# A two-layer mixer trunk on one core: the selection's last step moves to ScalarE, the first mean square to VectorE, and every operation gets a new place in the order

## The chip, the cores and the metric

The kernel runs on one core of a Trainium2 chip. The metric is the device time of one execution in microseconds (us), lower is better. The core has five engines with their own instruction queues: TensorE (PE in the profile; its weight loader is shown apart as PEld), VectorE (DVE), ScalarE (ACT), GpSimd (POOL) and SyncE (SP), which in this kernel issues nearly all transfers.

## The reference, cut to what matters

```python
D_MODEL, SEQ, DEPTH = 1024, 512, 2      # batch 1, float32

def rmsnorm(x, g):
    return x * lax.rsqrt(jnp.mean(x * x, axis=-1, keepdims=True) + EPS) * g

def dsa_mixer(q, k, v, qi, ki, wi):                     # group A, per block of 128 queries
    logits = einsum('bqhd,bsd->bqhs', qib, ki) * IDX_DIM ** -0.5
    score = einsum('bqhs,bqh->bqs', relu(logits), wib)  # 8 index heads
    score = where(causal, score, -inf)
    _, idx = lax.top_k(score, 128)                      # min(256, 512 // 4)
    s = einsum('bqhd,bqkd->bhqk', qb, k[idx]) * HEAD_DIM ** -0.5
    return einsum('bhqk,bqkd->bqhd', masked_softmax(s), v[idx])

def hybrid_layer(x, ...):
    p = split_cols(rmsnorm(x, norm_w) @ w_in)
    o_a = dsa_mixer(...)         # group A: indexer, top-k keys, softmax attention
    o_b = nsa_mixer(...)         # group B: compressed, selected and window attention
    o_c = shortconv_mixer(...)   # group C
    o_d = pool_mixer(...)        # group D
    mixed = concatenate([silu(gate) * o for each group])
    return x + mixed @ w_out

def reference(x, ...):
    for l in range(DEPTH):
        x = hybrid_layer(x, ...)
    return rmsnorm(x, final_norm_w)
```

## The kernel before

The 512 tokens are four tiles of 128 (index `i`, 0 to 3), the 1024 channels eight blocks of 128 (`KC`). Products are float32 done in three parts: each operand is split into a high half (ACT copy to the type fp32r) and a low half (DVE or POOL subtraction, the helper `lo` at L585), and TensorE multiplies high by high, high by low and low by high. So a weight block goes through SP (transfer into a staging tile `st`, four buffers), ACT (`wh`), POOL (`wl`; in the first block partly DVE) and then TensorE; `load_w` (L590) does that for `w_in`, `load_half` (L618) for the halves of `w_out`, whose two parts are both called `w`. The activations are `hT` (normed input, transposed, two halves) and `mT` (the mixed outputs, `mT_884` and `mT_885` the halves in layer 2).

A layer normalizes and transposes its input, projects it (`lin_tok`, `lin_ch`: PSUM banks called `mm`, two of them), runs the four groups, and projects the mixed channels with `w_out`, again into banks `mm`. The other PSUM banks are `s` (two: scores), `tr` (three: transposes) and `pv` (one: value products). In the last layer the residual add (`mm<-mm,x`), the scaling (`xn<-mm,g`) and the sum of squares (`junk<-mm`) read a bank `mm` before it is free for the next tile; `mm_1290` and `mm_1287` are the two column halves of one token tile there, `mm_1318` of the next.

The start (L766, `norm_first`): the first norm's two column halves of a token tile come as two loads of `x`. ACT squares and sums the one, DVE the other, POOL adds the two sums (`ss`) and takes the power -1/2 (`ss<-ss,mhalf`); DVE then scales `x` by quarters of 256 columns into `xn`, with the norm weight spread over the partitions by TensorE (`s<-ident,g_col`, L686), and TensorE transposes the quarters. POOL also fills the constants there (memsets and affine selects: `mask`, `cbias`, `cval`, `es`, `rg` and others).

Selection (L871 and L906, `group_idx` and `topk`): for the token tiles 1 to 3 the index score is built up over eight heads in `acc` (256, 384 or 512 wide). Then 16 rounds of DVE's `MAX8` and `MATCH_REPLACE8` mark the 128 largest by a very negative value, and one POOL instruction turns `acc` into 0 for the marked keys and -1e30 (`NEG`) for the others:

```python
            for _ in range(TOPK // 8):
                V.max(m8, a)
                V.match_replace(a, m8, a, MARK)
            G.tensor_scalar(a, a, -2.0e38, NEG, op0=OP.is_gt, op1=OP.mult)
```

`att_a` (L1172) gives it to `probs` (L1070), where one DVE instruction takes -0.125 times score and key bias together with the smallest element of each row (`pb`, `mn`), and ACT takes exp(-(p) + mn) with the row sums. The first token tile has no selection and uses the causal `mask`. Group B's attention uses `probs` and `probs_joint` too; its block selection goes over `e`, `el` (POOL and ACT), TensorE transposes and `es` (ACT).

What sets the order: nothing is issued as the functions run. `Tape.record` notes every operation with what it must follow, and `Tape.play` (L525) issues them in the sequence of a list written out in the code, `ORDER` (L179 to L447), one number for each of the recorded operations. Each engine gets its operations in that sequence, and `Tape.place` gives a tile the buffer of its pool that has been free longest in that sequence. That is why nearly every row of the profile has line L545, and why rows are told apart by their tiles.

Of the kernel before, what the change touches and what calls it, by code (L numbers as in the profile page):

```python
# [17 lines left out]
P = 128  # L18
# [152 lines left out]
class Engine:  # L171
# [378 lines left out]
def trunk(ctx: ExitStack, tc: tile.TileContext, x, norm_w, w_in, w_out, conv_w, pe_cmp, w_cmp_k, w_cmp_v,  # L550
# [31 lines left out]
    def f(ap):  # L582
        return ap.bitcast(F32)

    def lo(eng, dst, src, hi):  # L585

        eng.tensor_sub(dst, src, f(hi))
# [268 lines left out]
    def layer(l, hT, w_first, norm):  # L856
# [6 lines left out]
        def tk(i):  # L863
            return slice(i * P, (i + 1) * P)
# [607 lines left out]
```

## Time and profile before

| | us |
|---|---|
| runs of the kernel before | 528.71, 528.80, 530.26 |
| median | 528.8 |
| the profiled execution's own time | 530.93 |
| its span, first to last instruction | 528.9 |
| mean granted TensorE clock in it | 0.997 of full speed |

| engine | busy us | instructions |
|---|---|---|
| PE | 516.3 | 2887 |
| PEld | 437.9 | 2887 |
| DVE | 370.0 | 1024 |
| ACT | 332.6 | 821 |
| POOL | 330.8 | 596 |

A row of the timeline reads: start in us, length in us, engine, line, operation, output tile `<-` input tiles (without numbers), shapes, `x` count of instructions in a row, and in brackets the idle time before them with what ended it. A row of the groups reads: line, engine, operation, tiles and shape, count, then busy us and mean ns of one, then the idle time before them with what ended most of it. A row of the chain reads: start, length, what. A row of the waits reads: who waited for whom, total us, times, longest us. A matmul's row is longer than the distance to the next matmul's start, since they are pipelined.

### The profile page before, as it was taken

To read this page: it belongs to the slowest core of one execution; us is meant where nothing else is said; L and a number is where in the kernel's file an instruction comes from. 1 tells how busy PE (TensorE), PEld (TensorE's weight loads), DVE (VectorE), ACT (ScalarE), POOL (GpSimd) and SP (SyncE) were. 2 spreads that over 40 slices of the span, in tenths; PEclk is the share of its full clock that TensorE was granted. 3 is DMA by queue.
4 is the path that set the end of the run, shared out by engine and by line. 5 is a ranking of instruction groups with operands and counts; after the bars stand their busy time and mean duration, and the time that the engine had idled before them with its cause. 6 is when DMAs were issued, how large, how long until landed. Compare 5 with 4: busy or idle time off the path is not lost.

```text
span 528.9 us, 9309 instructions
## 1 busy us (share of the span) xinstructions
PE 516.3 (98%) x2887; PEld 437.9 (83%) x2887; DVE 370.0 (70%) x1024; ACT 332.6 (63%) x821; POOL 330.8 (63%) x596
## 2 busy tenths in 40 slices
PE   8999999999999999999999999999999999999995
PEld 8999988778888877788789998778888887878785
DVE  4525899899848575773453369999999856757523
ACT  5669954564466776774365788657475748675612
POOL 6887852776565946739276875457483876592531
PEclk9999999999999999999999999999999999999998
DMA  8943410763322111306543332165303212031304
GB/s 265 293 116 82 94 35 16 175 152 89 71 52 69 40 42 40 96 34 199 175 140 101 104 92 70 40 161 139 80 15 96 67 46 70 10 103 38 111 9 160
DMA packets 72993, 50.09 MB, mean 95 GB/s; under 512 B 24424, under 2 KB 63472, under 8 KB 72944
## 3 DMA queue, kind: packets, MB, share of 16 engines
q1 hardware_dynamic: 72352, 48.45, 33.7%
q10 hardware_dynamic: 592, 1.05, 0.5%
q8 instruction: 23, 0.38, 0.3%
q14 instruction: 26, 0.21, 0.1%
HBM read 45.29 MB, written 4.19 MB: 94 GB/s over the span
## 4 chain that ended last, share of the span: by engine, by line
PE 73%; DVE 9%; ACT 9%; POOL 3%; issue 2%; DMA 2%; SPq 1%; POOLq 0%; ACTq 0%; DVEq 0%
PE mm L545 53%; PE tr L545 9%; PE s L545 6%; PE pv L545 5%; DVE acc L545 2%; ACT qiT L545 2%; DVE m L545 1%; ACT pb L545 1%; ACT wh L545 1%; POOL cd L545 1%; DVE kTB L545 1%; DMA st<-in_w_out_dram 1%; POOL w L545 1%; SPq L545 1%; DMA x<-in_x_dram 1%
## 5 line engine op out<-in xcount | busy, mean ns | idle before, releaser
L545 PE MATMUL mm<-hT,wh 128*128 128x512 f32 x544 | 172.6, 399 | 0.5 <-ACT wh L545 0.5
L545 POOL TENSOR_TENSOR wl<-st,wh 128x384 fp32r<-128x384 f32 (+4 forms) x140 | 127.7, 936 | 32.8 <-ACT wh L545 25.3
L545 PEld LDWEIGHTS mm<-hT,wh 128*128 128x128 f32 x544 | 100.1, 188 | 20.2 <-ACT wh L545 1.0
L545 PE MATMUL mm<-w,mT 128*128 128x512 f32 (+1 forms) x408 | 101.7, 384 | 1.3 <-ACT junk L545 0.6
L545 PE MATMUL mm<-wh,hT 128*128 128x360 f32 (+3 forms) x480 | 100.5, 309 | 0.3 <-DVE vB L545 0.2
L545 PE MATMUL mm<-hT,wl 128*128 128x512 f32 x272 | 97.4, 401 | 0.2
L545 PEld LDWEIGHTS mm<-w,mT 128*128 128x128 f32 x408 | 71.9, 189 | 16.5 <-ACT junk L545 1.3
L545 PEld LDWEIGHTS mm<-wh,hT 128*128 128x128 f32 x480 | 76.5, 189 | 1.4 <-DVE vB L545 0.7
L545 ACT ACTIVATE wh<-st 128x768 fp32r<-128x768 f32 (+4 forms) x72 | 55.5, 780 | 19.4 <-DMA st<-in_w_in_dram 9.7
L545 ACT ACTIVATE pb<-pb,mn 128x128 f32<-128x128 f32 (+3 forms) x96 | 53.3, 557 | 21.3 <-DVE mn L545 20.5
L545 PE MATMUL mm<-wl,hT 128*128 128x360 f32 (+3 forms) x240 | 62.6, 310 | 0.0
L545 PEld LDWEIGHTS mm<-hT,wl 128*128 128x128 f32 x272 | 50.5, 188 | 9.9 <-POOL wl L545 0.5
L545 DVE MAX8 m<-acc 128x8 f32<-128x512 f32 (+2 forms) x96 | 51.7, 551 | 0.7
L545 DVE MATCH_REPLACE8 acc<-m,acc 128x384 f32<-128x384 f32 (+2 forms) x96 | 51.8, 542 | 0.1
L545 DVE TENSOR_TENSOR pl<-tr,ph 128x512 fp32r<-128x512 f32 x60 | 40.4, 684 | 15.7 <-ACT ph L545 9.3
L545 POOL TENSOR_SCALAR pb<-pb,rs,gt 128x512 f32<-128x512 f32 (+3 forms) x64 | 38.3, 615 | 20.6 <-DVE e L545 7.8
L545 POOL TENSOR_TENSOR w<-st,w 128x512 fp32r<-128x512 f32 x32 | 41.0, 1294 | 11.1 <-issue 7.1
L545 PEld LDWEIGHTS mm<-wl,hT 128*128 128x128 f32 x240 | 41.9, 189 | 0.9 <-ACT hT L545 0.3
L545 PE MATMUL tr<-ident,pb 128*128 128x128 f32 x240 | 41.5, 273 | 0.4 <-ACT es L545 0.4
L545 ACT ACTIVATE ph<-tr 128x512 fp32r<-128x512 f32 x60 | 34.3, 592 | 10.7 <-PE tr L545 10.4
L545 DVE CUSTOM_DVE_ANT_0 pb<-s,mask 128x128 f32<-128x128 f32 (+3 forms) x72 | 32.4, 461 | 10.5 <-PE tr L545 5.5
L545 PEld LDWEIGHTS tr<-ident,pb 128*128 128x128 f32 x240 | 30.5, 140 | 8.7 <-ACT es L545 0.6
(167 smaller groups left out, 867.9 us busy)
## 6 DMA issues: line engine op xcount, KB each, us to landing
st<-in_w_in_dram SPq DMA_DIRECT2D x104, 128.0 KB, 2.7
st<-in_w_out_dram SPq DMA_DIRECT2D x32, 256.0 KB, 3.0
st<-in_w_in_dram SPq DMA_DIRECT2D x28, 256.0 KB, 3.1
x<-in_x_dram SPq DMA_DIRECT2D x16, 256.0 KB, 4.8
st<-in_w_in_dram SPq DMA_DIRECT2D x8, 320.0 KB, 4.6
x1d<-x SPq DMA_DIRECT2D x8, 256.0 KB, 2.6
x<-x1d SPq DMA_DIRECT2D x8, 256.0 KB, 3.7
ws<-in_w_in_dram SPq DMA_DIRECT2D x4, 268.0 KB, 4.8
```

What stands on the lines that cost most here:

```text
L545: getattr(self.engines[op.eng].real, op.name)(*[real(a) for a in op.args], **{k: real(v) for k, v in op.kw.items()})
```

## The change

1. The last step of the selection is one ACT instruction, Relu(1e-8 a + 1e30): the marked keys become 0, the others 1e30, with the sign turned round. So group A's keys `kTA` are stored negated, `probs` takes +0.125 for group A, and the first token tile uses a new tile `hide` (0 or 1e30) in the place of a slice of `mask`. `far` is a new column of 1e30.
2. In `norm_first` DVE squares and sums both column halves, the second beginning with the sum of the first. ACT's Square and POOL's add go.
3. All of `ORDER` is new.

```diff
     mask = const.tile([P, T], F32, name="mask")
+    hide = const.tile([P, P], F32, name="hide")
...
     G.memset(mhalf, -0.5)
+    far = const.tile([P, 1], F32, name="far")
+    G.memset(far, -NEG)
...
         G.memset(cval, 1.0)
+        G.memset(hide, 0.0)
+        G.affine_select(hide, hide, pattern=[[-1, P]], compare_op=OP.is_ge, fill=-NEG, base=0, channel_multiplier=1)
...
-        S.activation(junk[0], xt[0], AF.Square, scale=DM**-0.5, accum_out=part[0])
-        V.tensor_tensor_reduce(out=junk[1], in0=xt[1], in1=xt[1], scale=1.0 / DM, scalar=EPS, op0=OP.mult, op1=OP.add,
-                               accum_out=part[1])
-        ms = part[0]
-        G.tensor_scalar(ms, ms, 1.0, part[1], op0=OP.mult, op1=OP.add)
+        for b in range(2):
+            V.tensor_tensor_reduce(out=junk[b], in0=xt[b], in1=xt[b], scale=1.0 / DM, scalar=part[0] if b else EPS,
+                                   op0=OP.mult, op1=OP.add, accum_out=part[b])
+        ms = part[1]
         G.tensor_tensor(ms, ms, mhalf, OP.pow)
...
-            G.tensor_scalar(a, a, -2.0e38, NEG, op0=OP.is_gt, op1=OP.mult)
+            S.activation(a, a, AF.Relu, scale=1.0e-8, bias=far)
...
-            S.activation(kTA[0][:, tk(i)], pq[:, 2 * P : 3 * P], AF.Copy)
-            lo(V, kTA[1][:, tk(i)], pq[:, 2 * P : 3 * P], kTA[0][:, tk(i)])
+            S.activation(kTA[0][:, tk(i)], pq[:, 2 * P : 3 * P], AF.Copy, scale=-1.0)
+            V.scalar_tensor_tensor(kTA[1][:, tk(i)], pq[:, 2 * P : 3 * P], -1.0, f(kTA[0][:, tk(i)]), op0=OP.mult,
+                                   op1=OP.subtract)
...
-                V.tensor_tensor_reduce(out=p, in0=ps[:, c : c + n], in1=bias, scale=-0.125, scalar=3.0e38,
+                V.tensor_tensor_reduce(out=p, in0=ps[:, c : c + n], in1=bias, scale=-0.125 if gcol else 0.125, scalar=3.0e38,
...
-            pb = probs("a", i, kTA, acc[i][:, :n] if i else mask[:, T - n :], None)
+            pb = probs("a", i, kTA, acc[i][:, :n] if i else hide, None)
```

The new list holds the same operations in nearly the same sequence, with most blocks shifted against each other by 0 to 2 us of TensorE's work. Three places of it follow.

SP, which issues the transfers, at the second half of layer 1's output weights (`st_6xx<-in_w_out_dram`). Before; `st_704` is a block of layer 2's input weights, `x_599` and `x_600` reload the input for the residual:

```order
L545 DMA st_653_3254<-in_w_out_dram 128x512
L545 DMA st_647_3269<-in_w_out_dram 128x512
L545 DMA st_644_3285<-in_w_out_dram 128x512
L545 DMA st_650_3297<-in_w_out_dram 128x512
L545 DMA st_643_3311<-in_w_out_dram 128x512
L545 DMA x_600_3313<-in_x_dram 128x512
L545 DMA st_704_3325<-in_w_in_dram 128x2x40
L545 DMA st_659_3337<-in_w_out_dram 128x512
```

After the change:

```order
L545 DMA st_653_3269<-in_w_out_dram 128x512
L545 DMA x_599_3271<-in_x_dram 128x512
L545 DMA st_647_3274<-in_w_out_dram 128x512
L545 DMA st_644_3322<-in_w_out_dram 128x512
L545 DMA st_650_3335<-in_w_out_dram 128x512
L545 DMA st_643_3342<-in_w_out_dram 128x512
L545 DMA st_659_3344<-in_w_out_dram 128x512
L545 DMA st_698_3348<-in_w_in_dram 128x2x320
```

The last block, `st_659`, follows `st_643` directly, and the next layer's weights and `x_600` come behind it; here the next layer's first block is `st_698`.

TensorE at the last projection, from the last matmul into the bank `mm_1290` to the first into `mm_1318`, which uses the same bank. Before:

```order
L545 MATMUL mm_1290_6312<-w_1275_6165,mT_884_5354 128x512
L545 MATMUL mm_1287_6345<-w_1272_6182,mT_884_5354 128x512
L545 MATMUL mm_1287_6345<-w_1274_6161,mT_884_5354 128x512
L545 MATMUL mm_1287_6345<-w_1280_6126,mT_884_5354 128x512
L545 MATMUL mm_1287_6345<-w_1280_6126,mT_885_5357 128x512
L545 MATMUL mm_1287_6345<-w_1265_6096,mT_884_5354 128x512
L545 MATMUL mm_1287_6345<-w_1262_5773,mT_884_5354 128x512
L545 MATMUL mm_1287_6345<-w_1274_6161,mT_885_5357 128x512
L545 MATMUL mm_1318_6472<-w_1295_6420,mT_885_5357 128x512
```

After the change, beginning with the matmul right behind the last one into `mm_1290`:

```order
L545 MATMUL mm_1287_6350<-w_1281_6281,mT_884_5360 128x512
L545 MATMUL mm_1287_6350<-w_1262_5759,mT_884_5360 128x512
L545 MATMUL mm_1287_6350<-w_1266_6135,mT_884_5360 128x512
L545 MATMUL mm_1287_6350<-w_1274_6164,mT_885_5371 128x512
L545 MATMUL mm_1287_6350<-w_1265_6104,mT_884_5360 128x512
L545 MATMUL mm_1287_6350<-w_1274_6164,mT_884_5360 128x512
L545 MATMUL mm_1287_6350<-w_1278_6168,mT_884_5360 128x512
L545 MATMUL mm_1287_6350<-w_1280_6133,mT_885_5371 128x512
L545 MATMUL mm_1287_6350<-w_1265_6104,mT_885_5371 128x512
L545 MATMUL mm_1287_6350<-w_1272_6234,mT_884_5360 128x512
L545 MATMUL mm_1287_6350<-w_1280_6133,mT_884_5360 128x512
L545 MATMUL mm_1318_6464<-w_1305_6402,mT_885_5371 128x512
```

Between the last matmul into `mm_1290` and the first into `mm_1318` stood seven matmuls into `mm_1287`, and eleven stand there now.

ACT behind layer 1's last selection. The tile `acc_174` is the 512-wide score; `pb_309` to `pb_312` are exponentials of group B, `cd` the convolution's input, `ph` a split of transposed probabilities. Before, where POOL did the last step of the selection:

```order
L545 ACTIVATE pb_311_2009,rg3_443<-pb_311_2009,mn_313_1935 128x512
L545 ACTIVATE tr_486_2012<-cd_485_1988 128x2
L545 ACTIVATE pb_312_2055,rg3_443<-pb_312_2055,mn_313_1935 128x512
L545 ACTIVATE cd_523_2070<-mm_522_1967 128x512
L545 ACTIVATE cd_521_2081<-mm_508_2032 128x512
L545 ACTIVATE ph_326_2109<-tr_325_2100 128x512
L545 ACTIVATE wh_535_2116<-st_534_2023 128x768
L545 ACTIVATE ph_320_2126<-tr_319_2104 128x512
```

After the change:

```order
L545 ACTIVATE pb_310_1982,rg3_108<-pb_310_1982,mn_313_1948 128x512
L545 ACTIVATE pb_312_2033,rg3_108<-pb_312_2033,mn_313_1948 128x512
L545 ACTIVATE cd_523_2065<-mm_522_1967 128x512
L545 ACTIVATE acc_174_1410<-acc_174_1410,far_102 128x512
L545 ACTIVATE cd_521_2083<-mm_508_2011 128x512
L545 ACTIVATE wh_535_2100<-st_534_2087 128x768
L545 ACTIVATE ph_326_2115<-tr_325_2108 128x512
L545 ACTIVATE ph_320_2131<-tr_319_2106 128x512
```

The selection's last step stands between the copies `cd_523` and `cd_521`, and what follows on ACT stands behind it.

At the start, SP now issues the two loads of the first token tile's `x` ahead of all weights, where a small weight transfer stood first; DVE copies the norm weight's column first and then takes both square passes; and POOL has 22 rows of fills and selects ahead of the first power -1/2 instead of 13. In group B's block selection for the third token tile of layer 2 the chain `el`, transposes, `es` stands earlier, its transposes by some 5 us of TensorE's work. The 256-wide selection's last step of layer 1 stood on POOL ahead of the low halves of the weights there, and stands on ACT now, behind the high halves `wh_270` and `wh_273`.

534 rows, old and new, of the table ORDER are left out of this document.

## The prediction

> **What bounds the kernel now.** I read the page first, its busy shares and its chain.
>
> ```profile
> PE 516.3 (98%) x2887; PEld 437.9 (83%) x2887; DVE 370.0 (70%) x1024; ACT 332.6 (63%) x821; POOL 330.8 (63%) x596
> PE 73%; DVE 9%; ACT 9%; POOL 3%; issue 2%; DMA 2%; SPq 1%; POOLq 0%; ACTq 0%; DVEq 0%
> ```
>
> TensorE bounds the kernel: it is marked busy for 98% of the span and holds 73% of the chain that ended last. The other engines have a third of their time free. The change leaves the matmuls as they are, so it can only win or lose the moments in which TensorE stands still, and the work ahead of its first and behind its last matmul. How many such moments there are is read from the waits of the weight loader, PEld, because a matmul's own row lasts past the start of the next one and hides short gaps (columns: total us, times, longest us; the three largest groups, and the one with the longest wait behind the start):
>
> ```profile
> PEld tr L545 <- issue: 3.3, 10, 0.6
> PEld s L545 <- DVE acc L545: 2.9, 8, 0.6
> PEld s L545 <- DVE mn L545: 2.1, 5, 0.8
> PEld mm L545 <- ACT junk L545: 1.3, 2, 1.1
> ```
>
> The largest group holds 3.3 us in ten pieces, and the longest single wait is 1.1 us. So there is no big thing to win. A difference of 0.3%, 1.6 us, is about what a measurement of this kernel can tell from no change.
>
> **The selection's last step.** Six POOL instructions go, two of each width, and six ScalarE activations come.
>
> ```profile
> L545 POOL TENSOR_SCALAR acc<-acc 128x512 f32<-128x512 f32 x2 | 3.9, 1926 | 0.2
> L545 POOL TENSOR_SCALAR acc<-acc 128x384 f32<-128x384 f32 x2 | 3.0, 1499 | 10.3 <-DVE acc L545 10.3
> L545 POOL TENSOR_SCALAR acc<-acc 128x256 f32<-128x256 f32 x2 | 2.2, 1091 | 0.2
> L545 ACT ACTIVATE pb<-pb,mn 128x512 f32<-128x512 f32 x24 | 17.2, 719 | 11.2 <-DVE mn L545 10.8
> L545 ACT ACTIVATE s<-s 128x512 f32<-128x512 f32 x16 | 9.3, 582 | 11.4 <-PE s L545 11.1 <-PE tr L545 0.2
> ```
>
> POOL loses 2 x (1926 + 1499 + 1091) ns = 9.0 us. No row shows a Relu from SBUF to SBUF; the nearest are the Exp of the same place and width, 719 ns, and the Relu in PSUM, 582 ns. I take the first, so a 512-wide step falls from 1.93 to about 0.72 us. On TensorE's path this matters at one place only, where the 256-wide step stands ahead of the weights' low halves on POOL and TensorE later waits for such a half:
>
> ```profile
> 98.60 1.09 POOL L545 TENSOR_SCALAR acc<-acc 128x256 f32<-128x256 f32 x1
> 104.98 0.30 PEld L545 LDWEIGHTS mm<-hT,wl 128*128 128x128 f32 x2 [0.55 <-POOL wl L545]
> 107.53 0.19 PEld L545 LDWEIGHTS s<-kTB,qb 128*128 128x128 f32 x1 [0.63 <-DVE mn L545]
> ```
>
> With 1.09 us off POOL's queue the 0.55 us wait can go whole; ScalarE, which must first write the high half, stands between, so I take 0.3 (0 to 0.55). At 107.53 the new order puts the first score block of that head group ahead of a selection step on DVE: 0.3 of 0.63. The negated keys cost eight DVE instructions a few ns each and the table `hide` two on POOL in the first stretch: nothing, with TensorE's other work as cover.
>
> **The last projection.** TensorE waits for the PSUM bank of `mm_1290`, which residual add, scaling and sum of squares must leave before `mm_1318` may start.
>
> ```profile
> 498.26 0.70 DVE L545 TENSOR_TENSOR mm<-mm,x 128x512 f32<-128x512 f32 x1 [1.43 <-PE mm L545]
> 499.72 0.60 ACT L545 ACTIVATE junk<-mm 128x512 bf16<-128x512 f32 x1 [0.90 <-DVE xn L545]
> 500.46 0.76 PEld L545 LDWEIGHTS mm<-w,mT 128*128 128x128 f32 x4 [1.06 <-ACT junk L545]
> 497.38 2.01 PEld L545 LDWEIGHTS mm<-w,mT 128*128 128x128 f32 x9
> ```
>
> The hand-over takes from 498.26 to 500.46 us. Nine loads in 2.01 us are 0.22 us for each matmul. The order had seven matmuls of `mm_1287` between the two banks and now has eleven: 4 x 0.22 = 0.9 us more cover. The loader's wait is 1.06, of which part lies under matmuls still running; I take 0.8 (0.4 to 1.0).
>
> **The second half of the output weights.** One block of layer 1 arrives late through a chain of buffer, transfer, ScalarE and POOL:
>
> ```profile
> 243.47 1.30 POOL w L545
> 248.89 3.96 DMA st<-in_w_out_dram
> 253.62 0.30 PEld L545 LDWEIGHTS mm<-w,mT 128*128 128x128 f32 x2 [0.50 <-ACT w L545]
> 254.97 0.99 PEld L545 LDWEIGHTS mm<-w,mT 128*128 128x128 f32 x5 [1.05 <-POOL w L545]
> ```
>
> The transfer waited on SP behind the next layer's weights and for a staging buffer that POOL had to leave. In the new order it follows its sister at once and takes a buffer that is free one POOL step, 1.30 us, sooner; TensorE asks for it about 4 matmuls, 0.9 us, sooner too. That leaves 0.4, and up to 0.4 more for the two transfers no longer ahead of it. I take 0.6 out of 1.55 (0 to 1.0). The next layer's weights, which now go behind it, have their use far off.
>
> **The second group's block selection in layer 2.** ScalarE's `es`, from which the value product of the selected blocks starts, was late by
>
> ```profile
> 439.73 0.14 PEld L545 LDWEIGHTS tr<-ident,pb 128*128 128x128 f32 x1 [0.63 <-ACT es L545]
> ```
>
> Its transposes now stand some 5 us sooner on TensorE, so the wait goes: 0.6 (0.4 to 0.6).
>
> **The start.** The first token tile's mean square is a chain over ScalarE, DVE and POOL:
>
> ```profile
> 2.27 0.43 SPq L545 DMA_DIRECT2D st<-in_w_in_dram  x1
> 4.05 0.69 DVE L545 CUSTOM_DVE_ANT_0 junk<-x 128x512 bf16<-128x512 f32 x1 [2.99 <-DMA x<-in_x_dram]
> 5.38 0.63 ACT L545 ACTIVATE junk<-x 128x512 bf16<-128x512 f32 x1 [2.66 <-DMA x<-in_x_dram]
> 6.64 0.55 POOL L545 TENSOR_TENSOR ss<-ss,mhalf 128x1 f32<-128x1 f32 x1
> 7.50 1.26 DVE L545 SCALAR_TENSOR_TENSOR xn<-x,ss,s 128x256 f32<-128x256 f32 x3 [2.58 <-POOL cval L545]
> 7.87 0.27 PE L545 MATMUL s<-ident,g_col 128*128 128x128 f32 x1
> 15.89 0.20 PEld L545 LDWEIGHTS tr<-ident,xn 128*128 128x128 f32 x2 [0.45 <-issue]
> ```
>
> ScalarE's pass and POOL's sum leave the chain, a second DVE pass of 0.69 us joins it, and the two loads of x now stand first on SP. ScalarE's pass began as the second load landed, at 5.38; that load now stands one place further ahead, and one issue on SP took 0.43. So it lands near 4.9, two passes of 0.69 one after the other end near 6.4, the power of 0.55 near 7.0, and the first scaled quarter begins some 0.4 us sooner than 7.50. But the third quarter also needs the spread norm weights, whose last piece ends at 7.87 + 0.27 = 8.14, and POOL has nine more fills ahead of the power than before. At 15.89 one fill no longer stands ahead of a sum. For both I take 0.2 (-0.5 to 0.75). For the other three token tiles DVE takes 0.69 us each from ScalarE, while TensorE has the first tile's products to do.
>
> The first and third of the next rows are POOL's, the others DVE's, and they bear on that chain:
>
> ```profile
> 8.24 0.95 POOL L545 TENSOR_TENSOR wl<-st,wh 128x360 fp32r<-128x360 f32 x1 [0.76 <-ACT wh L545]
> 8.68 0.90 DVE L545 TENSOR_TENSOR wl<-st,wh 128x360 fp32r<-128x360 f32 x1
> 12.59 0.52 POOL L545 TENSOR_SCALAR_AFFINE_SELECT cval<-cval 128x32 f32<-128x32 f32 x1
> 12.52 0.53 DVE L545 TENSOR_TENSOR wl<-st,wh 128x360 fp32r<-128x360 f32 x1
> ```
>
> The same DVE subtraction takes 0.90 us when it begins inside a POOL subtraction, and 0.53 us when it begins just ahead of a POOL select, which then takes 0.52 us for 32 columns. So where both read SBUF the later one waits. The Trainium skill ("SBUF — State Buffer", section "Who interferes with whom") states this as a rule: a DVE instruction with two SBUF inputs and a GpSimd instruction that reads SBUF shut each other out for a whole instruction, and the one issued first wins; these rows agree with it. By that rule the change is bad at the start, since both inputs of the new pass lie in SBUF beside POOL's selects, and good later on, since 9.0 us of POOL reads go.
>
> **What the new order costs.** The order moves nearly every block by 0 to 2 us of TensorE's work, and some producers come closer to their readers:
>
> ```profile
> 94.36 0.19 PEld L545 LDWEIGHTS s<-kiT,qiT 96*128 96x128 f32 x1 [0.34 <-DVE acc L545]
> 467.73 0.30 PEld L545 LDWEIGHTS tr<-cd,pw 128*128 128x128 f32 x2 [0.72 <-PE mm L545]
> ```
>
> Before the index products near 94.36 about 0.5 us of matmuls (two to three) go from between producer and reader, at 467.73 again about 0.46 us (two). A third place, a score block, loses one matmul, 0.23. If all came out as waits this were 1.2 us; DVE's share of the first comes back in part, and I take 0.9 (0 to 1.2). Other places where a producer comes closer show no idle time in this trace, so their waits can't be seen: I set two of the size of the row at 94.36, 0.34 each, so 0.7 (0 to 2).
>
> **The sum.** 0.8 + 0.6 + 0.6 + 0.3 + 0.3 + 0.2 = 2.8 us won, 0.9 + 0.7 = 1.6 lost, net -1.2. The profiled execution took 530.9 us (a span of 528.9 and 2.0 around it), 2.1 us above the median of the runs shown, 528.8; so 529.7 for its like after the change and 528.8 - 1.2 = **527.6 us** for the median.
>
> **The rivals.**
> *The order closes more than it opens.* Few single waits are above 0.3, and an order made anew may leave only those. With the upper bounds, 1.0 + 1.0 + 0.6 + 0.55 + 0.63 + 0.75 = 4.53 won and 0.9 lost, this gives 528.8 - 3.6 = 525.2; half way to the forecast, 526.4, is likelier. For it: the six places above are all helped. Against it: the bounds can't all be reached at once.
> *Nothing comes of it.* The edits touch engines that TensorE rarely waits for, and the rows that it waits for most often, index scores (`DVE acc`, 8 times) and score blocks (`DVE mn`, 5 times), are moved both ways. Each wait closed opens another, and the time is 528.8. This is also the case where the selection's step is cheaper but not on the path, and the first product waits for the spread norm weights.
> *A Relu stops ScalarE's queue.* This would make it slower. A Relu must wait for DVE's last pass, and what stands behind it on ScalarE waits too.
>
> ```profile
> POOL acc L545 <- DVE acc L545: 10.3, 2, 7.4
> 144.13 0.68 DVE L545 MATCH_REPLACE8 acc<-m,acc 128x512 f32<-128x512 f32 x1
> 144.44 0.60 ACT L545 ACTIVATE cd<-mm 128x512 f32<-128x512 f32 x1 [2.44 <-PE mm L545]
> 147.40 0.60 ACT L545 ACTIVATE ph<-tr 128x512 fp32r<-128x512 f32 x1 [2.36 <-PE tr L545]
> ```
>
> POOL waited up to 7.4 us for these passes. In layer 1 the widest Relu now stands ahead of `cd`; the last pass ends at 144.8, so `cd` would start at 144.8 + 0.7 = 145.5 instead of 144.44, 1.1 us late, and ScalarE's 2.36 us of idle time behind it takes that up. It decides from the point where DVE ends its passes more than about 1.3 us later against TensorE than now. With a wait as long as POOL's longest, 7.4 - 2.4 = 5.0 us reach the readers: 527.6 + 5.0 = 532.6; with half of that, 530.1.
> *The start loses to the shut-out.* The selects hold the passes, or the passes hold the selects and the power behind them, for one instruction, about 0.7 us: the start gives -0.5 instead of +0.2, so 528.3. By the Trainium skill's rule in the section named above this is what overlapping instructions would do.
>
> **How the numbers follow.** Forecast (526.8 to 528.5) 0.44, closing more 0.21, nothing 0.20, ScalarE stopped 0.09, the start's loss 0.06. Faster by over 0.3% is below 527.2: all of "closing more" and 0.18 of the forecast, 0.39. Slower is above 530.4: half of "ScalarE stopped" and some of "nothing" with more unseen waits, 0.10. Within 0.3%: 0.51. The range runs from the first rival's bound, 525.2, to 530.4, which leaves out the worst of the Relu's case.
>
> **What would show it.** In the profile after: the loader's wait for `ACT junk` near 500 us under 0.4; no wait for `POOL w` above 0.6 near 254; none for `ACT es` near 439; six ACT rows `acc<-acc` near 0.5 to 0.72 us and DVE's first scaled quarter near 7.1 us. Wrong would be: the idle time of the loader in sum no smaller than before (nothing comes of it), an ACT wait for `DVE acc` above 3 us with TensorE waiting for `wh`, `cd` or `ph` behind it, or a first product later than before.

## The result, and the profile after

| | before | after |
|---|---|---|
| median of the runs | 528.9 (528.71 to 530.26, 4 runs) | 524.25 (523.85 to 524.7, 4 runs) |
| ratio to the kernel before, 95% interval | | 0.9907 (0.9888 to 0.9926) |
| profiled execution: own time, span | 530.93, 528.9 | 523.85, 521.8 |

The change makes the kernel 4.65 us faster; the prediction said 1.2, with a lower end of 525.2. The page of the changed kernel, busy times and chain:

```profile
PE 511.8 (98%) x2887; PEld 438.7 (84%) x2887; DVE 371.1 (71%) x1026; ACT 332.0 (64%) x825; POOL 321.8 (62%) x592
PE 91%; DVE 4%; ACT 2%; issue 1%; DMA 1%; SPq 0%; POOL 0%; POOLq 0%; ACTq 0%
```

The work is the same, but TensorE now holds 91% of the chain that ended last, and 73% before: the other engines release it late less often. POOL's busy time fell by 9.0 us, as much as the six steps took. The weight loader's waits, the largest groups, and those that answer to the rows shown of before:

```profile
PEld s L545 <- DVE acc L545: 2.2, 7, 0.5
PEld tr L545 <- issue: 1.9, 7, 0.4
PEld mm L545 <- issue: 1.6, 7, 0.3
PEld tr L545 <- POOL ident L545: 1.5, 1, 1.5
PEld s L545 <- DVE mn L545: 1.3, 1, 1.3
...
PEld mm L545 <- ACT w L545: 0.3, 1, 0.3
...
PEld mm L545 <- ACT junk L545: 0.2, 1, 0.2
```

`ACT junk` fell from 1.3 to 0.2 us, `POOL w` and `ACT es` are gone from the view, and the five waits for `DVE mn` became one longer one. The timeline at the last projection of the changed kernel:

```profile
491.20 0.70 DVE L545 TENSOR_TENSOR mm<-mm,x 128x512 f32<-128x512 f32 x1 [1.29 <-PE mm L545]
492.66 0.60 ACT L545 ACTIVATE junk<-mm 128x512 bf16<-128x512 f32 x1 [2.16 <-DVE xn L545]
493.40 2.15 PEld L545 LDWEIGHTS mm<-w,mT 128*128 128x128 f32 x10 [0.15 <-ACT junk L545]
```

The hand-over of the bank still takes 2.2 us, 491.20 to 493.40, but TensorE has four more matmuls to do meanwhile and waits 0.15 us instead of 1.06.

Where the time went is seen stage by stage. For the table I took the start of each matmul from the traces and subtracted what the matmuls before it take back to back (0.229 us for 512 columns, 0.109 us for a 128 x 128 transpose, and so on): what is left is how long TensorE stood still. A stage runs between two fixed amounts of TensorE's work; its times are those of the first profile. The lengths subtracted are estimates: with others a stage's value moves by some tenths, 458-484 and 81-96 the most, while the sum over the whole span stays. "Again" is a second profile of the same kernel (e1 and e8 below). All values are us.

```
stage of the profile before    before  again   after  again
  1.5- 17  start                 3.74   3.43    3.62   4.03
 39 - 81   index score, layer 1  3.35   3.36    1.85   1.86
 81 - 96                         3.06   3.16    3.34   3.37
 96 -112                         1.36   0.83    0.42   1.71
112 -243                         4.20   4.13    3.73   3.71
243 -259   late output weights   1.34   2.04    0.12  -0.01
259 -290                         0.60   0.56    0.18   0.38
290 -338   index score, layer 2  3.09   3.08    2.22   2.22
338 -366                         3.02   3.39    3.50   3.50
427 -443   el, es                0.70   0.67    0.10   0.10
458 -484                         1.23   1.24    0.65   0.64
484 -505   last projection       1.23   1.27    0.28   0.26
```

Most stages repeat within 0.1 us from one execution to the next, so single profiles tell their causes (259-290 and 338-366 differ by up to 0.2 and 0.4). Three vary more: the start, 96-112 and 243-259. At 243-259 TensorE waits for weights that a transfer brings late. The 1.71 us at 96-112 are for the most part no wait: TensorE ran with half its clock there for 3.4 us (last section). In the first pair of profiles the named places (96-112, 243-259, 427-443, 484-505) gave 3.7 us, for 2.6 that the prediction had put on them; the rest comes from stages that it had put down as losses, the two index stages above all.

### The profile page after: what moved, and what is told of

It reads as the page before. It is cut to its first block, busy times and chain, and to the rows that moved or that the text cites. A ratio compares the mean times of both kernels' runs of the same rounds, so it can differ in the third digit from the quotient of the medians.

```text
span 521.8 us, 9310 instructions
## 1 busy us (share of the span) xinstructions
PE 511.8 (98%) x2887; PEld 438.7 (84%) x2887; DVE 371.1 (71%) x1026; ACT 332.0 (64%) x825; POOL 321.8 (62%) x592
## 4 chain that ended last, share of the span: by engine, by line
PE 91%; DVE 4%; ACT 2%; issue 1%; DMA 1%; SPq 0%; POOL 0%; POOLq 0%; ACTq 0%
PE mm L545 68%; PE tr L545 10%; PE s L545 7%; PE pv L545 6%; DVE acc L545 1%; DMA st<-in_w_in_dram 1%; DVE m L545 1%; ACT wh L545 1%; DVE kTB L545 1%; DVE mm L545 0%; DVE qiT L545 0%; ACT L545 0%; SPq L545 0%; ACT junk L545 0%; DVE pb L545 0%
## 5 line engine op out<-in xcount | busy, mean ns | idle before, releaser
L545 PE MATMUL mm<-hT,wl 128*128 128x512 f32 x272 | 100.1, 402 | 0.0
L545 PE MATMUL mm<-wh,hT 128*128 128x360 f32 (+3 forms) x480 | 99.2, 309 | 0.0
L545 ACT ACTIVATE pb<-pb,mn 128x512 f32<-128x512 f32 (+3 forms) x96 | 53.3, 557 | 15.5 <-DVE mn L545 15.1
L545 PE MATMUL mm<-wl,hT 128*128 128x268 f32 (+3 forms) x240 | 61.7, 307 | 0.0
L545 DVE CUSTOM_DVE_ANT_0 pb<-s,mask 128x512 f32<-128x512 f32 (+3 forms) x64 | 30.4, 485 | 9.4 <-PE s L545 4.7
```

The source lines that it names most:

```text
L545: getattr(self.engines[op.eng].real, op.name)(*[real(a) for a in op.args], **{k: real(v) for k, v in op.kw.items()})
```

## The experiments

All use the tables of operations of the two kernels. An order of the kernel before was carried over by giving the few added operations places beside their likes. The keys stay negated in all of them, so POOL's step, where it comes back, gives 0 or +1e30. Ratios stand to runs of the kernel before on the same chip.

**The kernel before once more**, unchanged.

> The kernel before, unchanged, profiled once more: how much of the 7.1 us between the two profiled spans belongs to the one execution that was profiled (530.93 us, 2.1 us above its median). If that execution was only a late one, this profile has a span near 526.8 us and the 2.1 us are missing at one or two places (the late output-weight transfer near 254 us, 1.3 us of TensorE standing still, is the first suspect). If all stalls of the first profile come back, the span is near 528.9 again and the loss lies in the kernel.

One run, 531.0 us, span 529.1: the stalls came back ("again" in the table). Both profiled executions of this kernel lie near the upper end of its runs (528.2 to 531.7 in all), so part of the 7.1 us between the spans is not in the medians. Which stalls the quicker runs lack can't be seen, as only profiled executions leave a trace.

**Order and edits apart.** The order alone takes both edits back, e4 the first one only:

```diff
-            S.activation(a, a, AF.Relu, scale=1.0e-8, bias=far)
+            G.tensor_scalar(a, a, -2.0e38, -NEG, op0=OP.is_gt, op1=OP.mult)
```

> The new order with the old operations: the selection's last step is on POOL, in the place where the Relu stands (keys still negated), and ScalarE squares the first half of x with POOL's add behind. Theory M (the order closes the stalls of TensorE, the edits are not on the path): 524.0 to 525.2 us. Rival E (the edits relieve POOL and the start, and the order only follows them): above 527 us.

> The old order with both edits: Relu on ScalarE at the place where POOL's step stood, both first square passes on VectorE. Theory M: 528 to 530 us, the same as before or a little slower where the Relu holds ScalarE's queue. Rival E: below 526 us.

> The changed kernel with only the selection's last step put back on POOL (same place in the order). If the Relu takes 1.1 to 1.9 us off the chain to the attention and off POOL's queue where TensorE waits, this is slower than the changed kernel by 0.3 us or more (524.6 to 526); by theory M it is within 0.4 us of it (524.0 to 524.7).

Measured: order only 532.58 us, ratio 1.005 (1.0035 to 1.0065); edits only 530.33, 1.0005 (0.9995 to 1.0015); the changed kernel with POOL's step 533.69, 1.0072 (1.0056 to 1.0089). Theory M failed as I had put it: the new order without the Relu is slower than the kernel before. But rival E failed as well, since the edits alone bring nothing. The timeline of e4 shows the largest part of the cause (its line numbers differ, since its table breaks its lines elsewhere):

```profile
145.02 1.92 POOL L557 TENSOR_SCALAR acc<-acc 128x512 f32<-128x512 f32 x1 [9.36 <-DVE acc L557]
147.04 3.02 POOL L557 TENSOR_SCALAR pb<-pb,rs,gt 128x512 f32<-128x512 f32 x4
150.11 0.14 PEld L557 LDWEIGHTS tr<-ident,pb 128*128 128x128 f32 x1 [4.96 <-POOL pb L557]
```

POOL reached the step long before VectorE's last pass, waited 9.36 us, and four weighted exponentials stood behind it; TensorE waited 4.96 us for them. Smaller waits for POOL are in e4 too (1.09 us for a low half at 101.33 us, 0.7 and 0.6 in layer 2), and from 150.74 us on, right behind the long one, the granted clock was 0.50 for 3.41 us. In the changed kernel the same step waits on ScalarE:

```profile
139.93 3.01 POOL L545 TENSOR_SCALAR pb<-pb,rs,gt 128x512 f32<-128x512 f32 x4 [5.77 <-ACT cd L545]
143.46 0.72 ACT L545 ACTIVATE acc<-acc,far 128x512 f32<-128x512 f32 x1 [3.65 <-DVE acc L545]
144.09 0.58 ACT L545 ACTIVATE cd<-mm 128x512 f32<-128x512 f32 x1
```

It holds ScalarE for 3.65 us there, and nothing that TensorE needs stands behind it; POOL's exponentials go by.

**The step on POOL, in places that suit it.** e4 with five of the six steps moved behind later POOL operations:

```
acc_134 behind wl_471, acc_174 behind pb_309, acc_776 behind wl_920,
acc_804 behind pb_981, acc_820 behind el_1041
```

> The new order with the selection's last step on POOL again, but five of the six steps moved further back in POOL's queue, each to a place where POOL stood idle in the changed kernel and its input was ready (the sixth stays). Theory Q (the step on POOL costs only because it stands in the queue and waits for VectorE's last pass, 9.4 us in the run before; the engine's time itself is free): the ratio to the kernel before is within 0.15% of the changed kernel's, that is about 0.990 to 0.993, and TensorE's 5.0 us wait for POOL's weighted exponentials is gone. Rival L (the 9 us of POOL's work and the longer step themselves count): 0.996 or more.

524.53 us, 0.9905 (0.9884 to 0.9926), beside 0.9908 (0.9887 to 0.993) of the changed kernel against the same runs, and the 5 us wait is gone. Theory Q holds: on POOL or on ScalarE, the last step costs the same time once it stands where it blocks nobody. So the gain comes with the order, and not with the engine of the step. The order must be fitted to the engine, though: the new list as it stands, with POOL's step, is the slow e4. The new first norm is still in e5; e12 below puts that back.

**The places apart.** Old operations in the old order, with the new one in the four stretches that were priced as gains (e6); the changed kernel with the old order in them (e7); the changed kernel again (e8):

> The old operations in the old order, except in four stretches of TensorE's work where the new order is followed: around 96 to 111 us (the low halves and the first score block), 243 to 259 (the late output weights), 427 to 443 (the block selection's es) and 484 to 505 (the last projection's bank) of the profile before. These are the places that the prediction priced as gains. The two profiles differ there by 0.95 + 1.22 + 0.60 + 0.95 = 3.7 us, so if places add up: 3.7 us below the kernel before in the profiled span, a ratio of 0.993 to 0.995. If the rival holds that closing these only shifts the wait: 0.998 or more.

> The changed kernel, but with the old order in those four stretches: what the prediction had put down as costs of the order, and as nothing. By the prediction's own term (0.9 + 0.7 us lost) it would be slower than the kernel before, a ratio of 1.002 to 1.004. By the difference of the two profiles outside the four stretches (3.4 us less standing still, most of it in the two stages where the index score is built up): 0.993 to 0.996.

> The changed kernel once more, on the same chip and beside the same runs of the kernel before as the three others: 0.9888 to 0.9926 by the interval already measured.

e6: 530.96 us, 1.0025 (1.0011 to 1.004), a miss; e7: 527.81, 0.9965 (0.9949 to 0.9981). In e6 the four stretches stand still for 1.43 us (0.49 + 0.59 + 0.06 + 0.29) instead of 4.63, which is 3.2 of the 3.7 expected. But right behind the cuts new stalls came: 0.9 us behind the last, 0.8 behind the third (1.47 where the kernel before has 0.65), 0.8 in the long stage between the first and the second. The start, which is the old one in code and order, was 0.8 us longer in this execution too. The first of these new stalls is the bank of the last projection again:

```profile
PEld mm L557 <- ACT junk L557: 1.1, 1, 1.1
```

TensorE had got ahead of the old order's next hand-over. So these four places, taken over without the rest, brought nothing. e7 settles the other side: what the prediction had booked as a loss is a gain of 0.35%, with the index stages at 1.88 and 2.20 us.

**Which engine's order makes the index stage.** The old order, with the new one in layer 1's index stage only: for all engines (e9), for TensorE alone (e10), for the others alone (e11).

> The changed operations in the old order, except in layer 1's first index stage (TensorE's work from about 39 to 81 us of the profile before), where all engines follow the new order. TensorE stood still there for 3.35 us before and for 1.85 us after. If the stage's own order makes the difference: 1.8 to 2.0 us in that stage, the stages behind it as before (within 0.3 us), and about 1.5 us off the span of the old order with the same operations. If it needs what stands around it: over 2.5 us in that stage.

> The same stage, but only TensorE follows the new order in it; VectorE, ScalarE and GpSimd keep theirs (ScalarE and SyncE but for a few places). Theory F (what counts is how many matmuls TensorE has between one head's score and the next): 1.8 to 2.3 us standing still in that stage. Theory C (what counts is how soon ScalarE and VectorE serve the chain score, Relu, accumulation): 3 us or more.

> The same stage, but only VectorE, ScalarE, GpSimd and SyncE follow the new order and TensorE keeps the old one. Theory C: 1.8 to 2.3 us standing still in that stage. Theory F: 3 us or more. If both this and the run with TensorE alone stay above 2.5 us, the two orders only work together.

TensorE stood still in the stage for 3.37 us in e3, 1.96 in e9, 7.49 in e10 and 6.38 in e11 (e10 took 534.87 us and e11 532.16, one execution each). (e9's time, 529.65 us, 0.9997 with 0.9982 to 1.0012, is no proof of 1.4 us; the next stage gave 0.56 of it back at the cut.) Both theories failed: half of the new order is worse than the old one. The weight loader's largest waits in the stage, in the kernel before, and then in e10 and e11:

```profile
PEld s L545 <- DVE acc L545: 0.7, 2, 0.5
PEld mm L545 <- DVE vB L545: 0.4, 1, 0.4
PEld mm L545 <- DVE vA L545: 0.4, 1, 0.4
PEld s L545 <- ACT qiT L545: 0.3, 1, 0.3
```

```profile
PEld s L557 <- DVE acc L557: 4.1, 7, 1.4
PEld mm L557 <- POOL wl L557: 1.2, 2, 0.6
```

```profile
PEld s L557 <- DVE acc L557: 1.9, 2, 1.7
PEld s L557 <- DVE qiT L557: 1.4, 1, 1.4
```

In e10 TensorE asks for scores earlier than VectorE accumulates them; in e11 VectorE is held up before results that TensorE makes later. What the new order does is to fit both: over the 48 heads of both layers the chain from score to accumulated `acc` takes 2.00 us on average after the change and 2.16 before, and the stalls right at the scores fall from 2.5 to 1.5 us.

**The edits one by one**, and the named places without a cut behind them. e12 and e13 put back the old first norm,

```diff
-        for b in range(2):
-            V.tensor_tensor_reduce(out=junk[b], in0=xt[b], in1=xt[b], scale=1.0 / DM, scalar=part[0] if b else EPS,
...
+        S.activation(junk[0], xt[0], AF.Square, scale=DM**-0.5, accum_out=part[0])
...
+        G.tensor_scalar(ms, ms, 1.0, part[1], op0=OP.mult, op1=OP.add)
```

e12 in the new order, e13 in the old; e14 has the new norm and POOL's step in the old order; e15 the changed operations in the old order, and the new one from 427 us on and at the two earlier places.

> The changed kernel with only the first mean square put back: ScalarE squares the first half of x, POOL adds the two sums. If the second edit pays (0.2 us by the prediction), 0.9911 to 0.9918 of the kernel before; if ScalarE's pass beside VectorE's is the quicker chain (its first scaled quarter began at 6.70 us in the run with the old operations, at 6.95 in the changed kernel), 0.9900 to 0.9908, and a faster kernel than both.

> The old order and the old first norm, with the selection's last step as Relu on ScalarE only. If the edits cancel in the run with both: three stalls closed (near 105, 255 and 440 us of the profile before; 0.9 + 0.6 us, and 0.4 to 1.0 at the second, which varies with a transfer), so 0.995 to 0.998 of the kernel before. If the Relu brings nothing on the path: 0.999 or more.

> The old order and POOL's selection step, with both first square passes on VectorE only. In the old order the copy of the norm weight's column stands behind both passes on VectorE; the run with both edits lost 4.9 us of TensorE's time in the first 17 us where the kernel before lost 3.4 to 3.7. If the edits cancel: 1.001 to 1.004 of the kernel before. If not: 0.999 to 1.001.

> The changed operations in the old order, but with the new order around 96 to 111 us, 243 to 264 us, and from 427 us to the end, so that no cut lies in the last stages. By the profiles TensorE stands still for 2.3 us less from 427 us on than in the old order (1.7 against 4.0 us), 0.6 of which the Relu alone already brings: 0.996 to 0.998 of the kernel before, or 1.7 us below the run with both edits in the old order. If stalls that are closed only come back behind: within 0.1% of the run with both edits in the old order.

e12: 524.06 us, 0.9899 (0.9876 to 0.9921); e13: 529.26, 0.9995 (0.9983 to 1.0007); e14: 532.15, 1.0054 (1.0035 to 1.0073); e15: 529.56, 1.0004 (0.9987 to 1.0021). The norm on VectorE alone loses, more than expected: 2.7 us, of which its profile shows about 1 at the start and 0.3 each at 290-338 and 458-484; the rest is not found. With Relu or without, TensorE stood still at the start for 4.9 and 4.8 us (e3, e14) with the new norm and for 3.6 (e13) with the old, in the old order; in the new order for 3.5 to 4.1 (e4, e5 and the changed kernel) against 2.6 and 2.9 (e2, e12). The start varies by about as much as this difference, but the two sets don't meet: over all profiles of the old order it is 3.4 to 4.5 us with the old norm and 4.6 to 5.8 with the new. The start in e12:

```profile
4.42 0.63 ACT L557 ACTIVATE junk<-x 128x512 bf16<-128x512 f32 x1 [1.72 <-DMA x<-in_x_dram]
4.62 0.68 DVE L557 CUSTOM_DVE_ANT_0 junk<-x 128x512 bf16<-128x512 f32 x1
5.77 0.26 POOL L557 TENSOR_SCALAR ss<-ss,ss 128x1 f32<-128x1 f32 x1
6.12 0.56 POOL L557 TENSOR_TENSOR ss<-ss,mhalf 128x1 f32<-128x1 f32 x1
6.71 1.26 DVE L557 SCALAR_TENSOR_TENSOR xn<-x,ss,s 128x256 f32<-128x256 f32 x3 [1.39 <-POOL ss L557]
```

and in the changed kernel:

```profile
4.63 0.69 DVE L545 CUSTOM_DVE_ANT_0 junk<-x 128x512 bf16<-128x512 f32 x1
5.37 0.75 DVE L545 CUSTOM_DVE_ANT_0 junk<-x,ss 128x512 bf16<-128x512 f32 x1
6.28 0.56 POOL L545 TENSOR_TENSOR ss<-ss,mhalf 128x1 f32<-128x1 f32 x1 [0.52 <-DVE ss L545]
6.95 0.87 DVE L545 SCALAR_TENSOR_TENSOR xn<-x,ss,s 128x256 f32<-128x256 f32 x2 [0.82 <-POOL ss L545]
8.41 0.48 DVE L545 SCALAR_TENSOR_TENSOR xn<-x,ss,s 128x256 f32<-128x256 f32 x1 [0.59 <-PE s L545]
```

Two engines side by side are ready 0.24 us sooner, sum and all, than one engine twice. Then the third quarter waits for TensorE's spread norm weights in the changed kernel; in e12 these came sooner, for a reason told at the end, so the whole difference isn't the edit's. So e12 is the best version on the table by its median, but its interval lies across that of the changed kernel, so it isn't shown to be faster. e13 missed: its profile has the stalls near 105 and 440 us closed and 0.8 us left at 243-259, yet its time is that of the kernel before. Against the two profiles of before it stands still 2.0 us less; against the medians nothing. Most of the 2.0 lies in the three stages that vary; without them it is 0.5 us, which its interval (0.9 us faster to 0.4 slower) holds. e15 missed in time too: from 427 us on it stood still for 1.7 us, as expected, instead of 4.0 before and 3.5 in e3, but it lost 0.9 against e3 at the start, whose code and order are the same (its transposes ran slowly until 10.07 us, in e3 until 5.55; last section), and 0.6 behind the cut at 112 us.

## Why the prediction was wrong

The step that failed is the term **"What the new order costs"**: 0.9 us for three places where producers came closer, and 0.7 for places unseen. What it stands for came out as a gain of about 3 us in the profiles: 1.5 and 0.9 in the index stages, 0.6 at 458-484, 0.5 at 112-243 and 0.3 at 259-290, against 0.2 lost at 81-96 and 0.3 at 338-366. The two index stages are the firm part; the smaller ones are near what the estimate of the lengths can tell. e7 confirms the sign in time, 0.9965. The fault is in how the term was made. I counted the matmuls that stand between a producer and its reader and held the producer's chain at its old length. The clearest miss is 467.73: two matmuls less, priced as a wait of 0.46, and no wait there at all in the changed kernel (a wait of 0.26 us for VectorE's `cd` follows 1 us later). e10 and e11 show why counting one side tells nothing: with TensorE's new order and the others' old one the stage gets 4.1 us worse, with both it gets 1.4 better.

Point by point:

- TensorE bounds the kernel and the only thing to win is its standing still: right. The profile pair accounts for the whole difference of spans in this way.
- The last projection, 0.8: right (1.23 to 0.28 us in its stage).
- The output weights, 0.6 (0 to 1.0): the mechanism is a transfer whose landing varies. Nine traces in the old order stood still there for 0.03 to 2.04 us, 0.92 on average, and eight in the new for -0.01 to 0.86, 0.42. So 0.5, as priced, though the first pair of profiles shows 1.2.
- The block selection, 0.6: the size was right, and the cause given is enough, but it is not the only one. e6 keeps POOL's step and follows the new order there: the transposes of `el` stand at 430.93 us instead of 436.20, and the wait is gone (0.06 in the stage). In the old order the Relu alone closes it as well (0.06 in e13). Before, POOL's 1.93 us step stood ahead of POOL's work on `cd`, for which ScalarE waited, and `es` stands behind that on ScalarE:

```profile
428.37 1.93 POOL L545 TENSOR_SCALAR acc<-acc 128x512 f32<-128x512 f32 x1
430.38 1.96 POOL L545 TENSOR_SCALAR pb<-pb,rs,gt 128x384 f32<-128x384 f32 x3
436.14 0.60 ACT L545 ACTIVATE tr<-cd 64x512 f32<-64x512 f32 x1 [2.99 <-POOL cd L545]
437.62 0.60 ACT L545 ACTIVATE tr<-cd 64x512 f32<-64x512 f32 x1 [0.88 <-POOL cd L545]
438.24 0.38 ACT L545 ACTIVATE es<-tr 64x256 fp32r<-64x256 f32 x1
```

So the claim that POOL's step mattered "at one place only" was wrong. That it matters is a question of what stands behind it, not of its 9.0 us.
- The low halves near 105 us and the score block near 107: closed, 0.9 in the one profile of before and 0.3 in the other, by the Relu alone; priced at 0.6. The score block's wait is in the first profile only.
- The Relu's duration: estimated 0.72 us for 512 columns, measured 0.72 (0.62 and 0.49 for the narrower).
- The start, 0.2: nothing in sum, made of a loss of about 1 us by the second edit and a gain of somewhat less by the new order (3.6 to 2.6 and 2.9 with the old norm); that it comes from the loads of `x` was not tried alone. The first scaled quarter began at 6.95 us, as forecast (7.1), but the third waited until 8.41 for the spread norm weights, which the prediction had named as the other limit. I also priced the edit for all four token tiles; the function is called for the first alone, as the rows of `junk<-x` on ACT after 8 us show. The shut-out of VectorE and POOL that was a rival is not seen: the two passes took 0.69 and 0.75 us beside POOL's fills, which read nothing. The Trainium skill's rule on shared ports ("SBUF — State Buffer", section "Who interferes with whom") has no instance there.
- The rival of a Relu that stops ScalarE: the wait came, 3.65 us, where the prediction had it, and cost nothing, since ScalarE's own idle time took it up, as priced. The same wait on POOL cost 5 us in e4: the mechanism was real, on the other engine.
- The range ended at 525.2, with closing more than opening as a rival at 0.21. The result was this rival's, beyond its bound, because the bound still held the 0.9 us of costs and no gain outside the named places. That its bounds add up to 4.53 us, near the 4.65 measured, is luck: the start gave nothing, and about 3 us came from stages that it didn't name.

Open: which stalls the quicker runs of the kernel before lack. Without the start, 96-112 and 243-259 the stages of the table and between them sum up to 4.8 us less (means of the two profiles each; 4.0 to 5.2 with other estimates of the matmuls' lengths), close to the measured 4.65, but that fit isn't a proof. No run shows in time what a single stage is worth: e9, with layer 1's index stage alone, stood still 1.4 us less in it and was not measurably faster.

## What to carry to other kernels

A hand-written order is one fitted whole: four stretches of it gave a slower kernel (1.0025), one gave no measurable gain (0.9997), and one engine's part of a stage, or all others' without it, made that stage worse (7.5 and 6.4 us instead of 3.4). To price a new order, follow the chain of producers with its new places on every engine before setting a wait; counting the work in front of the reader alone gave the wrong sign. An instruction that must wait costs what stands behind it in its queue, so it should go to the engine, or the place, where nothing urgent follows.

## What the runs showed of the hardware

TensorE's granted clock changes within an execution, and in a count of idle time the loss looks like a wait. TensorE's small transposes at the start run at two speeds, and the change from the slow to the fast one comes at another moment in each execution of one kernel. The same four transposes in the timelines of the two profiled executions of the kernel before, the first and then e1:

```profile
5.76 1.06 PE L545 MATMUL s<-ident,g_col 128*128 128x128 f32 x4
```

```profile
5.76 0.74 PE L545 MATMUL s<-ident,g_col 128*128 128x128 f32 x4
```

The trace's record of the granted clock begins at full speed at 7.17 us in the one and at 6.03 in the other, and these are the moments from which a transpose starts 0.11 us behind the one before it instead of 0.21. The last of the `g_col` transposes ended at 8.14 us in the one and at 7.59 in the other; in the changed kernel, whose record begins at 7.18 us, it ended at 8.38, and in e12, with 5.03, at 7.32. The latest moment is e15's, 10.07 us, and its start is the longest.

The clock can also fall later. These are the clock rows (tenths of full speed, in 40 slices of the span) of the changed kernel, of e8, which is the same kernel, and of e12:

```profile
PEclk9999999999999999999999999999999999999998
PEclk9999999899999999999999999999999999999999
PEclk9999999799999999999999999999999999999999
```

From 95.98 to 99.39 us in e8, and from 93.77 to 100.60 in e12, the granted clock was 0.50, and a 512-column matmul started 0.43 us behind the one before it instead of 0.23. Half of these stretches, 1.7 and 3.4 us, is lost; that is the second profile's 1.71 us at 96-112 but for some tenths. e2 and e4 have such a stretch of 3.41 us about the end of their 5 us wait, and e2 another near 95 us. The ten profiles that keep the old order in most stages have none before the last 5 us of the span. In time: the three runs of e8 with a mean clock of 0.995 or 0.996 took 525.37 to 525.68 us, the three with 0.997 or 0.998 took 524.12 to 524.24. What makes the clock fall in one execution and not in another of the same kernel was not tried. The clock, and the landing of transfers near 243-259 us, is what can be seen here of the 0.5% by which runs of one kernel differ.
